# The gating projection with the inner dimension outermost: x loaded transposed, eight PSUM banks, small loads behind the large ones

## The chip, the cores and the metric

One Trainium2 chip, one of its cores. The metric is the device time of one execution in microseconds (us); shorter is better. Times inside the kernel are counted from the start of the span of a profiled execution.

## The reference, cut to what matters

One layer of a streaming encoder over 1024 frames of 1024 channels. The change touches the first projection alone, columns 0 to 511 of `w_in`, and how its operands reach the chip.

```
h    = rms_norm(x, norm_mix)                 # x: 1024 x 1024
proj = h @ w_in                              # 1024 x 2304
z_sgu, z_s5, z_qkv = split(proj, [512, 768])
o_a = sgu_mixer(gelu(z_sgu), ...)            # spatial gating: u * (W v + b), v = rms_norm(...)
o_b = s5_mixer(z_s5, lam, log_dt, b, c, ...) # diagonal state space, its powers made of lam and dt
o_c = band_attention(q, k, v, ...)
x   = x + rms_norm(concat[o_a, o_b, o_c]) @ w_out
x   = x + hier_moe(rms_norm(x))              # 16 experts
```

## The kernel before, in words

The program is one straight line. Python code emits instructions tile by tile; a scheduler then sets, when the program is built, the order in which each engine takes its instructions, by dependencies and program order. On the chip each engine takes its list in that order: an instruction that waits holds up those behind it on its engine. Up to the attention no order is written out by hand.

Matrix products in float32 are made of three passes (`mm3`, L129 to L132): an operand a is split into a high part (ScalarE copy to the short float, `split` L126) and a low residual (VectorE subtraction, L127), and high times high, high times low and low times high are summed in PSUM.

The first projection (`sgu_proj`, L190 to L223) goes over eight blocks `tb` of 128 frames, in pairs `pr`. For a pair, TensorE transposes 16 tiles of 128 x 128 of x against an identity matrix (L205, into `hTp`, PSUM tag `big`, three buffers of two banks). ScalarE turns `hTp` into the high part `hTh` with the gain (L209) and VectorE makes the residual `hTl` (L210). Then one block is one accumulation over all eight slices k of the inner dimension (24 matmuls of 512 columns) into one bank `pj` of the tag `acc` (two buffers of one bank), and ScalarE evicts it through GELU with the frame's scale `rs` into `gz` (L195). The scale comes from the squares of x (ScalarE, L218) and a short VectorE iteration (`rsqrt`).

Loads are issued from the SyncE queue: two blocks of x, the four pieces of the weight (`rw`, L173), six more blocks of x. Eight small loads go through ScalarE's queue. Each DMA uses one of eight completion counters in turn and waits for the one that used it before.

Behind the projection in program order stand:
- `r8` (L229 to L234): a one-column-block matmul `rsp` of `rs`, copied by VectorE. It orders the scales for the state space part.
- the preparation of the state space part (L308 to L434), some 60 VectorE instructions on `lam`, `dt`, `s5c`, `ak`, `scr`, `kap`, `bcm`, with two sines (L359) and two exponentials (L317, L376) on ScalarE, each of which has its own function table to load.
- the state space projection (four accumulations `pj` of 24 matmuls, evicted as `zT` by ScalarE, L446).
- the gating itself (`sgu`, L249 to L289), a generator whose pieces are emitted between those accumulations: VectorE sums (L259) and normalises `gz` into `vn` (L263), ScalarE and VectorE split it into `vh` and `vl`, TensorE multiplies with the mask weights `wsh` into `sgup` (12 matmuls, L270), VectorE forms `oa` (L275). It runs twice (`tq`).
- the k, q and v projections, between which the state space scan (`s5`) is emitted, attention, the output product, the experts.

Of the kernel before, what the change touches and what calls it, by code (L numbers as in the profile page):

```python
# [4 lines left out]
F32 = mybir.dt.float32  # L5
# [9 lines left out]
S = 1024  # L15
D = 1024
# [15 lines left out]
def trunk(tc, A, dbg=None, upto="all"):  # L32
# [35 lines left out]
    def slot(name, shape, dt=F32, far=None):  # L68
        far = name in FAR if far is None else far
        return slots.tile(shape, dt, name=name, tag="far" if far else "slot", bufs=FARS if far else SLOTS)  # L70
# [4 lines left out]
    def big(name, shape, dt=F32):  # L75
        return psum.tile(shape, dt, name=name, tag="big", bufs=3)

    def acc(name, shape, dt=F32):
        return psum.tile(shape, dt, name=name, tag="acc", bufs=2)
# [19 lines left out]
    def f32(ap):  # L99
        return ap.bitcast(F32)  # L100
# [37 lines left out]
    def load_x(tb):  # L138
        t = slot("xt", [128, D])
        sp.dma_start(t, x[tb * 128:(tb + 1) * 128, :])  # L140
        return t
# [6 lines left out]
    def junk():  # L148
        return work.tile([128, D], BF, name="junk", tag="w2")
# [17 lines left out]
    def load_w(c0, n, far=()):  # L167

        his, los = [], []
        per = 1024 // n  # L170
        for r in range(KD // per):
            rw = raw("rw", [128, per, n])
            sp.dma_start(rw, w_in[r * per * 128:(r + 1) * per * 128, c0:c0 + n]  # L173
                         .rearrange("(k p) c -> p k c", p=128))
            h = slot("wh", [128, per, n], F32R, far=r in far)
            l = slot("wl", [128, per, n], F32R, far=r in far)
            split(h, l, rw)
            his += [h[:, i] for i in range(per)]
            los += [l[:, i] for i in range(per)]
        return his, los  # L180

    def proj(out, sel, w, ks=range(KD)):
        his, los = w
        for k in ks:
            mm3(out, hT[k][:, sel], lT[k][:, sel], his[k], los[k], k == ks[0], k == ks[-1])

    gz = []
    rs = const("rs", [128, NT])

    def sgu_proj(tb):  # L190
        a = acc("pj", [128, 512])
        proj(a, slice(tb * 128, (tb + 1) * 128), W["sgu"])
        if tb % 2 == 0:
            gz.append(slot("gz", [128, 2, 512]))
        act.activation(gz[tb // 2][:, tb % 2], a, AF.Gelu_apprx_tanh, scale=rs[:, tb:tb + 1])  # L195

    W = {}
    xs = {0: load_x(0), 1: load_x(1)}
    for pr in range(4):
        for kq in range(2):  # L200
            p = big("hTp", [128, 4, 256])
            for q in range(2):
                for k in range(4):
                    kk = 4 * kq + k
                    pe.transpose(p[:, k, q * 128:(q + 1) * 128], xs[2 * pr + q][:, kk * 128:(kk + 1) * 128], ident)  # L205
            for k in range(4):
                kk = 4 * kq + k
                sl = slice(pr * 256, (pr + 1) * 256)
                act.activation(hT[kk][:, sl], p[:, k], AF.Copy, scale=gmix[:, kk:kk + 1])  # L209
                dve.scalar_tensor_tensor(lT[kk][:, sl], p[:, k], gmix[:, kk:kk + 1], f32(hT[kk][:, sl]),  # L210
                                         op0=OP.mult, op1=OP.subtract)
        if pr == 0:
            W["sgu"] = load_w(0, 512)
            for tb in range(2, NT):
                xs[tb] = load_x(tb)
        ss = small.tile([128, 2], F32, name="ssx")
        for q in range(2):
            act.activation(junk(), xs[2 * pr + q], AF.Square, accum_out=ss[:, q:q + 1])  # L218
        rsqrt(rs[:, 2 * pr:2 * pr + 2], ss, 2, 1.0 / D)
        if pr == 3:  # L220
            W["s5"] = load_w(512, 256)
        sgu_proj(2 * pr)
        sgu_proj(2 * pr + 1)  # L223
    W["k"] = load_w(1280, 512)

    div8, mod8 = const("div8", [128, 16]), const("mod8", [128, 8])
# [10 lines left out]
    row256 = const("row256", [128, 256])  # L237
    gsgu, glub = row256, row256
    wsr = slot("wsr", [128, 4, 128])
    act.dma_start(gsgu, bass.AP(tensor=A["sgu_norm"].tensor, offset=A["sgu_norm"].offset, ap=[[0, 128], [1, 256]]))  # L240
    sgb = const("sgb", [128, 4])
    act.dma_start(sgb, A["sgu_bT"])
    act.dma_start(wsr, A["sgu_wT"])
    pool.memset(wsr[64:128, :, 0:64], 0.0)
    wsh = slot("wsh", [128, 2, 4, 128], F32R)
    split(wsh[:, 0], wsh[:, 1], wsr)
# [58 lines left out]
            v = v.rearrange("p (a b c) -> p a b c", a=shape[1], b=shape[2])  # L305
        return v

    lam = const("lam", [128, 2, NG])  # L308
    act.dma_start(lam, A["lam2"])
    ldt = const("ldt", [128, NG])  # L310
    act.dma_start(ldt, bass.AP(tensor=A["log_dt"].tensor, offset=A["log_dt"].offset, ap=[[0, 128], [1, NG]]))
    bc_in = slot("bc_in", [128, 4, NG, 16])
    act.dma_start(bc_in, A["bc2"])
    d5 = const("d5", [16, NG])
    act.dma_start(d5, A["s5_dT"])
    dt = const("dt5", [128, NG])
    act.activation(dt, ldt, AF.Exp)  # L317
    th = const("th5", [128, NG])
# [310 lines left out]
    W["q"] = load_w(768, 512, (0, 1))  # L629
    qt_ = qk_proj("qt", W["q"])  # L630
    W["v"] = load_w(1792, 512, (3,))
    gqk = const("gqk", [128, 2])
    act.dma_start(gqk, A["qk2"])
    gq = const("gq", [128, 1])
    dve.scalar_tensor_tensor(gq, gqk[:, 0:1], 64 ** -0.5, gqk[:, 1:2], op0=OP.mult, op1=OP.mult)

# [969 lines left out]
def layout(inputs):  # L1606

    import numpy as np
    i = {k: np.asarray(v) for k, v in inputs.items()}
    f = np.ascontiguousarray  # L1610
    o = {"x": i["x"], "w_in": i["w_in"][0]}
    lr, li = i["s5_lambda_re"][0].T, i["s5_lambda_im"][0].T
    o["lam2"] = np.stack([np.concatenate([lr, lr]), np.concatenate([li, li])], 1)
    br, bi = (i[n][0].transpose(1, 0, 2) for n in ("s5_b_re", "s5_b_im"))
    cr, ci = (i[n][0].transpose(2, 0, 1) for n in ("s5_c_re", "s5_c_im"))
    o["bc2"] = np.stack([np.concatenate(p) for p in ((br, bi), (bi, br), (cr, ci), (ci, cr))], 1)
    o["log_dt"] = i["s5_log_dt"][0]
    o["s5_dT"] = i["s5_d"][0].reshape(16, 16).T
    o["glu_w"] = i["s5_glu_w"][0]
    o["glu_b"] = i["s5_glu_b"][0]  # L1620
    o["sgu_norm"] = i["sgu_norm"][0]
    o["sgu_bT"] = i["sgu_b"][0].T
    o["sgu_wT"] = i["sgu_w"][0].transpose(2, 0, 1)
    o["qk2"] = np.stack([np.concatenate([i[n][0]] * 2) for n in ("q_norm", "k_norm")], 1)
    o["norm_ffn"] = i["norm_ffn"][0]
    o["gT"] = np.stack([i[n][0].reshape(8, 128).T for n in ("norm_mix", "out_norm", "norm_ffn")], 1)
    o["w_out"] = i["w_out"][0]
    o["w_router"] = np.concatenate([i["router_group_w"][0], i["router_expert_w"][0].transpose(1, 0, 2).reshape(D, 16)], 1)
    o["b_router"] = np.concatenate([i["router_group_b"][0], i["router_expert_b"][0].reshape(16)])
    o["w_gu"] = np.concatenate([i["w_gate"][0], i["w_up"][0]], 2)  # L1630
    o["w_down"] = i["w_down"][0]
    rb = i["rel_bias"][0]
    rx = np.concatenate([np.repeat(rb[:, 512:], 639 - 255, axis=1), rb[:, 129:512][:, ::-1]], axis=1)

    o["relT"] = np.stack([rx[:, 127 - q:767 - q] for q in range(128)], 1)
    return {k: f(v) for k, v in o.items()}
# [17 lines left out]
```

## Time and profile before

| | |
|---|---|
| three runs | 831.81, 834.27, 837.59 us (median 834.27) |
| the profiled execution | 835.0 us, its span 833.1 us |
| TensorE busy | 755.7 us, 91% of the span |
| VectorE busy | 530.1 us, 64% |
| ScalarE busy | 400.9 us, 48% |
| GpSimd busy | 200.4 us, 24% |
| moved by DMA | 111.31 MB, 134 GB/s over the span |

A span runs from the first to the last instruction; the execution's own time is 1.9 us longer. In the rows further down, a timeline row gives start, duration, engine, line, operation, tiles and shape, and in brackets how long the engine had been idle and which instruction ended that. Matmuls are pipelined: the distance between two starts is what one costs, not its duration. PE is TensorE, DVE VectorE, ACT ScalarE, POOL GpSimd, SPq SyncE's queue.

### The profile page before, as it was taken

The numbers are of one execution on the slowest core, as the hardware profiler recorded it, in microseconds if no ns is written. First come the engines' busy times: TensorE is split into PE (matmuls) and PEld (weight loads), VectorE is DVE, ScalarE is ACT, GpSimd is POOL, SyncE is SP. The second block draws the span as 40 slices with busy tenths as digits, with TensorE's granted clock in tenths as the row PEclk, the third lists the DMA queues.
The fourth block names the chain that finished last, engine by engine and source line by source line (L and its number), as shares of the span: only waits on it lengthen the run. The fifth ranks groups of instructions, "written<-read, shape, count | busy, mean of one in ns | idle before, by whom it ended". The sixth has DMA issues, their size and how long they took to land. (4 is left out here: it accounts for less than half of the span.)

```text
span 833.1 us, 13661 instructions
## 1 busy us (share of the span) xinstructions
PE 755.7 (91%) x5024; PEld 640.0 (77%) x5025; DVE 530.1 (64%) x1266; ACT 400.9 (48%) x751; POOL 200.4 (24%) x235
## 2 busy tenths in 40 slices
PE   5999998989999887888888999968899999999995
PEld 4878777868888777888887888747678778888884
DVE  5866799873651467787877544677675774575541
ACT  6763432223343467777774323434454654464441
POOL 0000245411410332212101121112242433243221
PEclk9999999999999989999999999998999999999998
DMA  8423011330000400001045323286889999899663
GB/s 312 138 57 102 6 15 15 54 114 0 2 1 1 126 26 2 1 27 52 2 132 188 140 101 127 76 306 201 286 283 279 328 349 315 223 308 309 130 154 54
DMA packets 56516, 111.31 MB, mean 134 GB/s; under 512 B 24272, under 2 KB 28880, under 8 KB 56432
## 3 DMA queue, kind: packets, MB, share of 16 engines
q1 hardware_dynamic: 46880, 84.14, 30.0%
q0 software_dynamic: 6480, 23.60, 11.9%
q10 hardware_dynamic: 3072, 2.49, 1.0%
q8 instruction: 47, 0.77, 0.4%
q14 instruction: 37, 0.30, 0.1%
HBM read 90.05 MB, written 20.17 MB: 132 GB/s over the span
## 5 line engine op out<-in xcount | busy, mean ns | idle before, releaser
L130 PE MATMUL pj<-wh,hTh 128*128 128x512 f32 x256 | 104.2, 408 | 0.4 <-ACT hTh L209 0.3
L131 PE MATMUL pj<-wl,hTh 128*128 128x512 f32 x256 | 101.6, 397 | 0.0
L132 PE MATMUL pj<-wh,hTl 128*128 128x512 f32 x256 | 100.5, 398 | 0.1
L130 PE MATMUL gup<-gh,hgh 128*128 128x256 f32 x304 | 89.8, 295 | 1.7 <-ACT hgh L1278 0.2
L132 PE MATMUL gup<-gh,hgl 128*128 128x256 f32 x304 | 86.8, 286 | 3.1 <-DVE hgl L1282 3.1
L131 PE MATMUL gup<-gl,hgh 128*128 128x256 f32 x304 | 86.0, 283 | 0.0
L1325 PE MATMUL yp<-rwd,hh 128*128 128x256 f32 (+1 forms) x264 | 84.4, 457 | 0.0
L977 DVE TENSOR_TENSOR gl<-rwg,gh 128x1024 fp32r<-128x1024 f32 x64 | 78.0, 1241 | 7.3 <-ACT gh L972 6.5
L972 ACT ACTIVATE gh<-rwg 128x1024 fp32r<-128x1024 f32 x64 | 64.1, 1052 | 1.4 <-ACTq L1581 0.4
L1325 PEld LDWEIGHTS yp<-rwd,hh 128*128 128x128 f32 x264 | 45.8, 190 | 23.2 <-issue 17.4
L130 PEld LDWEIGHTS gup<-gh,hgh 128*128 128x128 f32 x304 | 57.9, 191 | 6.1 <-ACT y L1334 5.2
L132 PEld LDWEIGHTS gup<-gh,hgl 128*128 128x128 f32 x304 | 58.2, 191 | 4.5 <-DVE hgl L1282 3.6
L131 PEld LDWEIGHTS gup<-gl,hgh 128*128 128x128 f32 x304 | 58.2, 191 | 0.1
L132 PEld LDWEIGHTS pj<-wh,hTl 128*128 128x128 f32 x256 | 48.1, 188 | 12.7 <-DVE hTl L210 1.3
L130 PEld LDWEIGHTS pj<-wh,hTh 128*128 128x128 f32 x256 | 48.5, 190 | 12.0 <-ACT hTh L209 1.3
L1337 POOL DMA_INDIRECT out<-y,ix x22 | 38.2, 1735 | 78.9 <-ACT y L1334 45.9
L127 DVE TENSOR_TENSOR ptl<-ps,pth 128x640 fp32r<-128x640 f32 (+2 forms) x53 | 39.7, 749 | 26.5 <-ACT pth L126 26.1
L131 PEld LDWEIGHTS pj<-wl,hTh 128*128 128x128 f32 x256 | 48.4, 189 | 10.4
L130 PE MATMUL po<-pth,v_h 128*64 128x128 f32 x236 | 47.8, 232 | 2.9 <-DVE oc L765 2.0
L1334 ACT ACTIVATE y<-yp 128x512 f32<-128x512 f32 (+1 forms) x44 | 21.6, 491 | 59.6 <-PE yp L1325 59.6
L1262 POOL DMA_INDIRECT hg<-h2d,ix x22 | 23.8, 1080 | 105.2 <-PE yp L1325 69.5
L732 PE MATMUL ps<-ident,st 128*128 128x128 f32 x240 | 38.5, 290 | 9.8 <-ACT st L723 9.2
(390 smaller groups left out, 1974.9 us busy)
## 6 DMA issues: line engine op xcount, KB each, us to landing
rwg<-in_w_gu SPq DMA_DIRECT2D x62, 512.0 KB, 9.0
rwd<-in_w_down SPq DMA_DIRECT2D x32, 512.0 KB, 6.6
rw<-in_w_in SPq DMA_DIRECT2D x18, 512.0 KB, 5.1
xt<-in_x SPq DMA_DIRECT2D x8, 512.0 KB, 9.2
rwo<-in_w_out SPq DMA_DIRECT2D x8, 512.0 KB, 4.6
xr<-in_x SPq DMA_DIRECT2D x8, 512.0 KB, 4.3
out<-x SPq DMA_DIRECT2D x8, 512.0 KB, 2.6
h2d<-h SPq DMA_DIRECT2D x8, 512.0 KB, 2.9
```

The source lines that it names most:

```text
L127: (eng_lo or dve).tensor_tensor(lo, src, f32(hi), op=OP.subtract)
L130: pe.matmul(out, ah, bh, start=first, stop=False)
L131: pe.matmul(out, ah, bl, start=False, stop=False)
L132: pe.matmul(out, al, bh, start=False, stop=last)
L732: pe.transpose(pp[:, b], st[:, b * 128:(b + 1) * 128], ident)
L972: act.activation(pc[1], pc[0], AF.Copy)
L977: eng.tensor_tensor(t, pc[0], f32(pc[1]), op=OP.subtract)
L1262: pool.indirect_dma_start(out=self.hg, out_offset=None, in_=h2d[:, :], in_offset=bass.IndirectOffsetOnAxis(ap=self.ix, axis=0))
L1325: pe.matmul(self.py[nb][0], self.hh[r], self.ex.d[r][:, ns], start=(r == 0), stop=(r == 1))
L1334: act.activation(self.y[:, ns], p, AF.Copy)
L1337: pool.indirect_dma_start(out=out[:, :], out_offset=bass.IndirectOffsetOnAxis(ap=self.ix, axis=0), in_=self.y, in_offset=None, compute_op= ...
```

## The change

The host lays x out a second time, transposed (`xT`). The projection then needs no transposes: slices of `xT` come by DMA, and `hTh`, `hTl` are made from SBUF. The loop over the inner dimension becomes the outer one: for each slice k all eight blocks `tb` are advanced by three matmuls, so that eight accumulations are open at once, in all eight PSUM banks (three buffers of `big` with two banks each, two of `acc`). GELU evictions follow at the end. x itself is loaded after the transposed copy, for the squares alone. The small loads move from ScalarE's queue to SyncE's, behind the large ones.

```
-    gz = []
+    gz = [slot("gz", [128, 2, 512]) for _ in range(NT // 2)]
-    def sgu_proj(tb):
-        a = acc("pj", [128, 512])
-        proj(a, slice(tb * 128, (tb + 1) * 128), W["sgu"])
...
-        act.activation(gz[tb // 2][:, tb % 2], a, AF.Gelu_apprx_tanh, scale=rs[:, tb:tb + 1])
-    xs = {0: load_x(0), 1: load_x(1)}
-    for pr in range(4):
-        for kq in range(2):
-            p = big("hTp", [128, 4, 256])
...
-                    pe.transpose(p[:, k, q * 128:(q + 1) * 128], xs[2 * pr + q][:, kk * 128:(kk + 1) * 128], ident)
...
-        sgu_proj(2 * pr)
-        sgu_proj(2 * pr + 1)
+    pj = [big("pj", [128, 2, 512]) for _ in range(3)]
+    pj = [t[:, i] for t in pj for i in range(2)] + [acc("pj", [128, 512]) for _ in range(2)]
+    for r in range(4):
+        rw = raw("rw", [128, 2, 512])
+        sp.dma_start(rw, w_in[r * 256:(r + 1) * 256, 0:512].rearrange("(k p) c -> p k c", p=128))
+        xT = []
+        for k in (2 * r, 2 * r + 1):
+            xT.append(slot("xt", [128, S]))
+            sp.dma_start(xT[-1], A["xT"][k * 128:(k + 1) * 128, :])
+        wh, wl = slot("wh", [128, 2, 512], F32R), slot("wl", [128, 2, 512], F32R)
+        for i in range(2):
+            k = 2 * r + i
+            g = gmix[:, k:k + 1]
+            split(wh[:, i], wl[:, i], rw[:, i])
+            for sl in (slice(0, 512), slice(512, S)):
+                act.activation(hT[k][:, sl], xT[i][:, sl], AF.Copy, scale=g)
+                dve.scalar_tensor_tensor(lT[k][:, sl], xT[i][:, sl], g, f32(hT[k][:, sl]), op0=OP.mult, op1=OP.subtract)
+            for tb in range(NT):
+                sel = slice(tb * 128, (tb + 1) * 128)
+                mm3(pj[tb], hT[k][:, sel], lT[k][:, sel], wh[:, i], wl[:, i], k == 0, k == KD - 1)
+    lam = const("lam", [128, 2, NG])
+    sp.dma_start(lam, A["lam2"])
...
+    bc_in = slot("bc_in", [128, 4, NG, 16])
+    sp.dma_start(bc_in, A["bc2"])
...
+    for tb in range(NT):
+        act.activation(junk(), load_x(tb), AF.Square, accum_out=ss[:, tb:tb + 1])
+    rsqrt(rs, ss, NT, 1.0 / D)
+    W["s5"] = load_w(512, 256)
+    for tb in range(NT):
+        act.activation(gz[tb // 2][:, tb % 2], pj[tb], AF.Gelu_apprx_tanh, scale=rs[:, tb:tb + 1])
     W["k"] = load_w(1280, 512)
...
-    act.dma_start(wsr, A["sgu_wT"])
+    sp.dma_start(wsr, A["sgu_wT"])
...
-    gqk = const("gqk", [128, 2])
-    act.dma_start(gqk, A["qk2"])
+    gqk = small.tile([128, 2], F32, name="gqk", tag="s16")
+    sp.dma_start(gqk, A["qk2"])
...
-    o = {"x": i["x"], "w_in": i["w_in"][0]}
+    o = {"x": i["x"], "xT": i["x"][0].T, "w_in": i["w_in"][0]}
```

The scheduler sets new orders for the first part of the program; from the transposes `s5u` on, TensorE, ScalarE and GpSimd have the same list as before, and VectorE too but for one small multiplication (`gq`) that has moved between two weight splits of the v projection. Three places follow. The numbers behind the names are buffers; what stands in brackets is which engines or DMA counters an instruction waits for.

VectorE, before, around the copy of `r8` (the end of the first projection): `bcm`, the last of the state space preparation, and the residuals `hTl` stand ahead of it, the first sums of the gating (ISA on `gz`) right behind.

```order
L420 TENSOR_TENSOR bcm_704<-bcm_704,s5c_621 128x256 [waits DVE_49]
L127 TENSOR_TENSOR wl_521<-rw_518,wh_520 128x1024 [waits DMAHW5_49,Activation_49]
L210 SCALAR_TENSOR_TENSOR hTl0_92<-hTp_459,gains_82,hTh0_84 128x256 [waits Activation_49]
...
L127 TENSOR_TENSOR wl_592<-rw_589,wh_591 128x1024 [waits DMAHW3_49,PE_49,Activation_49]
L234 COPY r8_609<-rsp_607 128x8 [waits PE_49]
L127 TENSOR_TENSOR wl_598<-rw_595,wh_597 128x1024 [waits DMAHW4_49,Activation_49]
L259 ISA vn_755,sv_753<-gz_219 128x256
```

VectorE, now, around the same copy, and where the gating's first sum stands:

```order
L231 TENSOR_TENSOR rsx_485<-rs_104,div8_481 128x128 [waits DVE_49]
L127 TENSOR_TENSOR wl_446<-rw_443,wh_445 128x1024 [waits DMAHW2_49,Activation_49]
L235 COPY r8_489<-rsp_487 128x8 [waits PE_49]
L342 TENSOR_TENSOR s5c_501<-tH_517,kio_522 128x144 [waits Pool_49]
L127 TENSOR_TENSOR wl_460<-rw_457,wh_459 128x1024 [waits DMAHW3_49,Activation_49]
L127 TENSOR_TENSOR wsh_498<-wsr_492,wsh_498 128x512 [waits DMAHW1_49,Activation_49]
...
L343 TENSOR_SCALAR s5c_501<-s5c_501 128x144 [waits DVE_49]
...
L412 TENSOR_TENSOR s5c_501<-kap_557,bc_in_386 128x256 [waits DVE_49]
L260 ISA vn_627,sv_625<-gz_100 128x256
```

Three of the four weight splits of the k projection, the split of `wsh` and 48 instructions of the preparation (from L342 to L412) have moved from ahead of the copy of `r8` to between it and the gating, where the fourth weight split stood before, too.

ScalarE, before, from the end of the first projection's GELU evictions on (the sines and exponentials stood between earlier evictions):

```order
L126 ACTIVATE wh_591<-rw_589 128x1024 [waits DMAHW3_49,PE_49]
L195 ACTIVATE gz_549<-pj_551,rs_100 128x512 [waits PE_49]
L126 ACTIVATE wh_597<-rw_595 128x1024 [waits DMAHW4_49]
L446 ACTIVATE zT0_725<-pj_727 128x512 [waits PE_49]
L126 ACTIVATE vh_756<-vn_755 128x1024 [waits DVE_49]
```

and now:

```order
L224 ACTIVATE gz_103<-pj_109,rs_104 128x512 [waits PE_49]
L126 ACTIVATE wh_459<-rw_457 128x1024 [waits DMAHW3_49]
L126 ACTIVATE wsh_498<-wsr_492 128x512 [waits DMAHW1_49,Pool_49]
...
L352 ACT_TABLE_LOAD
L352 ACTIVATE ak_527<-ak_527 128x288 [waits DVE_49]
L352 ACTIVATE scr_539<-scr_539 128x768 [waits DVE_49]
L369 ACT_TABLE_LOAD
L369 ACTIVATE s5c_501<-s5c_501 128x144 [waits DVE_49]
L439 ACTIVATE zT0_597<-pj_599 128x512 [waits PE_49]
L439 ACTIVATE zT0_597<-pj_676 128x512 [waits PE_49]
L126 ACTIVATE vh_628<-vn_627 128x1024 [waits DVE_49]
```

The sines and the exponential of the preparation now stand behind all evictions and ahead of the first `zT`.

TensorE, before, at the first product of the gating (`sgup`), in the third accumulation of the state space projection:

```order
L130 MATMUL pj_879<-hTh0_84,wh_514 128x512 [waits Activation_49]
L131 MATMUL pj_879<-hTl0_92,wh_514 128x512
L132 MATMUL pj_879<-hTh0_84,wl_515 128x512
L130 MATMUL sgup_782<-vh_756,wsh_618 128x256 [waits PE_49,Activation_49]
L130 MATMUL pj_879<-hTh1_85,wh_514 128x512
```

and now, at the same place:

```order
L130 MATMUL pj_751<-hTh6_90,wh_445 128x512
L131 MATMUL pj_751<-hTl6_98,wh_445 128x512
L130 MATMUL sgup_654<-vh_628,wsh_498 128x256 [waits Activation_49]
L132 MATMUL pj_751<-hTh6_90,wl_446 128x512
L130 MATMUL pj_751<-hTh7_91,wh_445 128x512
L131 MATMUL pj_751<-hTl7_99,wh_445 128x512
L132 MATMUL pj_751<-hTh7_91,wl_446 128x512
L130 MATMUL pj_819<-hTh0_84,wh_439 128x512
L131 MATMUL sgup_654<-vl_629,wsh_498 128x256 [waits DVE_49]
```

The first `sgup` has moved from behind the 51st matmul of that projection to behind the 68th.

## Rows read from the trace of the kernel before

**Rows 1.** The page, busy us (share of the span) and instructions of TensorE.

```profile
PE 755.7 (91%) x5024; PEld 640.0 (77%) x5025; DVE 530.1 (64%) x1266; ACT 400.9 (48%) x751; POOL 200.4 (24%) x235
```

**Rows 2.** Timeline of TensorE, the first projection, and the state space projection's first matmul.

```profile
9.90 3.67 PE L205 MATMUL hTp<-ident,xt 128*128 128x128 f32 x16 [9.90 <-DVE ident L146]
...
25.80 2.79 PE L205 MATMUL hTp<-ident,xt 128*128 128x128 f32 x24
...
50.40 0.39 PE L132 MATMUL pj<-wh,hTl 128*128 128x512 f32 x1
50.63 0.39 PE L130 MATMUL pj<-wh,hTh 128*128 128x512 f32 x1
...
65.97 0.28 PE L232 MATMUL rsp<-mod,rsx 128*128 128x8 f32 x2
66.91 0.51 PE L130 MATMUL pj<-hTh,wh 128*128 128x512 f32 x1 [0.66 <-ACT gz L195]
```

**Rows 3.** DMA issues from 0 to 1 us and from 1 to 2 us: median us to landing.

```profile
xt<-in_x SPq DMA_DIRECT2D x1, 512.0 KB, 3.8
...
xt<-in_x SPq DMA_DIRECT2D x2, 512.0 KB, 4.4
```

**Rows 4.** Timeline of VectorE, preparation of the state space part, then the gating.

```profile
36.00 0.30 DVE L355 TENSOR_TENSOR ak<-s5c 128x144 f32<-128x144 f32 x1
...
37.21 0.56 DVE L349 TENSOR_TENSOR s5c<-tH,cio 128x384 f32<-128x384 f32 x1
...
42.35 0.31 DVE L375 TENSOR_TENSOR s5c<-lr,kio 128x144 f32<-128x144 f32 x1
...
45.88 0.17 DVE L377 COPY rad<-s5c 128x16 f32<-128x16 f32 x1 [1.15 <-ACT s5c L376]
...
52.64 0.41 DVE L420 TENSOR_TENSOR bcm<-bcm,s5c 128x256 f32<-128x256 f32 x1
...
63.88 3.50 DVE L127 TENSOR_TENSOR wl<-rw,wh 128x1024 fp32r<-128x1024 f32 x3 [4.89 <-ACT wh L126]
...
68.98 0.42 DVE L259 CUSTOM_DVE_ANT_0 vn<-gz 128x256 f32<-128x256 f32 x1
...
75.46 1.23 DVE L127 TENSOR_TENSOR vl<-vn,vh 128x1024 fp32r<-128x1024 f32 x1 [1.13 <-ACT vh L126]
81.52 2.16 DVE L275 SCALAR_TENSOR_TENSOR oa<-sgup,sgb,gz 128x128 f32<-128x128 f32 x8 [4.84 <-PE sgup L132]
```

**Rows 5.** Timeline of ScalarE, sine, table load, exponential, weight splits, last eviction, `vh`.

```profile
43.00 0.84 ACT L359 ACTIVATE scr<-scr 128x768 f32<-128x768 f32 x1
...
44.23 1.28 ACT L376 ACT_TABLE_LOAD   x1
45.52 0.33 ACT L376 ACTIVATE s5c<-s5c 128x144 f32<-128x144 f32 x1
...
62.80 2.94 ACT L126 ACTIVATE wh<-rw 128x1024 fp32r<-128x1024 f32 x3
66.17 0.69 ACT L195 ACTIVATE gz<-pj,rs 128x512 f32<-128x512 f32 x1 [0.43 <-PE pj L132]
...
74.37 1.06 ACT L126 ACTIVATE vh<-vn 128x1024 fp32r<-128x1024 f32 x1 [1.03 <-DVE vn L263]
```

**Rows 6.** Timeline of TensorE, first matmul of both gating products; the scan's longest wait.

```profile
78.72 0.28 PE L130 MATMUL sgup<-vh,wsh 128*128 128x256 f32 x1
...
92.54 0.39 PE L130 MATMUL sgup<-vh,wsh 128*128 128x256 f32 x1 [1.72 <-ACT vh L126]
...
141.37 0.49 PE L546 MATMUL s5y<-w,f 128*128 128x128 f32 x2 [3.71 <-DVE w L538]
```

**Rows 7.** Windows: busy PE, PEld, DVE, ACT, POOL; granted clock; DMA share; GB/s.

```profile
142.00:143.00 1.00, 1.00 (x7) 1.00 (x6) 1.00 (x2) 0.00 (x0) 0.00 (x0) 0.50 0.00 0
...
145.00:146.00 1.00, 1.00 (x10) 1.00 (x9) 0.90 (x3) 0.25 (x1) 0.69 (x3) 0.90 0.00 0
...
100.00:110.00 10.00, 10.00 (x61) 8.48 (x60) 8.78 (x17) 6.75 (x17) 4.39 (x5) 1.00 0.01 2
```

More of the change, by code (lines that the diff above doesn't have):

```diff
@@ L185, in proj @@
             mm3(out, hT[k][:, sel], lT[k][:, sel], his[k], los[k], k == ks[0], k == ks[-1])
-    gz = []
+    gz = [slot("gz", [128, 2, 512]) for _ in range(NT // 2)]
     rs = const("rs", [128, NT])
-    def sgu_proj(tb):
-        a = acc("pj", [128, 512])
-        proj(a, slice(tb * 128, (tb + 1) * 128), W["sgu"])
-        if tb % 2 == 0:
-            gz.append(slot("gz", [128, 2, 512]))
-        act.activation(gz[tb // 2][:, tb % 2], a, AF.Gelu_apprx_tanh, scale=rs[:, tb:tb + 1])
-    W = {}
@@ L198, in trunk @@
-    xs = {0: load_x(0), 1: load_x(1)}
-    for pr in range(4):
-        for kq in range(2):
-            p = big("hTp", [128, 4, 256])
-            for q in range(2):
-                for k in range(4):
-                    kk = 4 * kq + k
-                    pe.transpose(p[:, k, q * 128:(q + 1) * 128], xs[2 * pr + q][:, kk * 128:(kk + 1) * 128], ident)
[L206 to L221, printed above, removed]
-        sgu_proj(2 * pr)
-        sgu_proj(2 * pr + 1)
@@ new lines, in trunk @@
+    lam = const("lam", [128, 2, NG])
+    sp.dma_start(lam, A["lam2"])
+    ldt = const("ldt", [128, NG])
+    sp.dma_start(ldt, bass.AP(tensor=A["log_dt"].tensor, offset=A["log_dt"].offset, ap=[[0, 128], [1, NG]]))
+    bc_in = slot("bc_in", [128, 4, NG, 16])
+    sp.dma_start(bc_in, A["bc2"])
+    d5 = const("d5", [16, NG])
+    sp.dma_start(d5, A["s5_dT"])
+    ss = const("ssx", [128, NT])
+    for tb in range(NT):
+        act.activation(junk(), load_x(tb), AF.Square, accum_out=ss[:, tb:tb + 1])
@@ L239, in trunk @@
     wsr = slot("wsr", [128, 4, 128])
-    act.dma_start(gsgu, bass.AP(tensor=A["sgu_norm"].tensor, offset=A["sgu_norm"].offset, ap=[[0, 128], [1, 256]]))
+    sp.dma_start(gsgu, bass.AP(tensor=A["sgu_norm"].tensor, offset=A["sgu_norm"].offset, ap=[[0, 128], [1, 256]]))
     sgb = const("sgb", [128, 4])
-    act.dma_start(sgb, A["sgu_bT"])
-    act.dma_start(wsr, A["sgu_wT"])
+    sp.dma_start(sgb, A["sgu_bT"])
+    sp.dma_start(wsr, A["sgu_wT"])
     pool.memset(wsr[64:128, :, 0:64], 0.0)
@@ L306, in tmp @@
         return v
[L308 to L315, printed above, removed]
     dt = const("dt5", [128, NG])
```

## The prediction

> **What bounds the kernel now.** The page comes first: TensorE is busy for 91% of the span [rows 1], so what counts is when each stage of it can begin. Then its timeline at the start. It does nothing until 9.90 us, transposes, and ends the first projection at 65.97 [rows 2]. The 192 matmuls of that projection start 0.233 us apart (50.40 to 50.63) [rows 2], which makes 44.8 of the 56.1 us; the rest is transposes and a slow beginning. What the reader is to see next is that VectorE's timeline in the same stretch is not idle: the state space preparation (`s5c` to `bcm`, 36.00 to 52.64) runs there, under the projection's matmuls, and is over before the gating's first sum at 68.98 [rows 4]. So two chains end near 69 us: TensorE's, which the change shortens, and VectorE's, which it reorders. The question is which is late afterwards.
>
> **What the change removes on TensorE.** Of the 64 transposes the first 16 fill 9.90 to about 13.3 [rows 2], 0.21 us each; the other 48 cost 2.79/24 = 0.116 each [rows 2], 5.6 us. Now the first matmul needs one weight piece and one slice of `xT`. The first load of 512 KB took 3.8 us from its issue at 0.75, and the pair in flight had a median of 4.4, so the second took 5.0 from about 1.2 [rows 3]: they landed near 4.6 and 6.2. The new order is weight piece, slice, slice, with no small loads in between; I take 4.6 and 5.9. ScalarE's half slice (0.6 us, the size of an eviction [rows 5]) gives a first matmul at about 6.65, VectorE's residual a steady run from 7.35. TensorE begins at the lower of its two levels (1.2 GHz), as behind its wait at 141.37, where the granted clock was 0.50 at 142 and 0.90 on the mean of 145 to 146, so low for about 3.8 us [rows 6, 7]. By 10.4 some 8 matmuls are done, and 184 x 0.233 = 42.9 put the end, call it T, at **53.4**, 12.6 us before 65.97. Later slices come faster than they are used: a slice and its half of a weight piece are one and a half loads, 2.4 us by that spacing of 1.6, and feed 24 matmuls, 5.6 us. Range of T: 52 to 55.5 by the landing.
>
> **What it moves on VectorE and ScalarE.** VectorE's list has the copy of `r8` right behind `rsx`. That copy waits for the matmul `rsp`, which stands behind the whole projection on TensorE. Everything behind it on VectorE, the preparation included, therefore waits for T, although VectorE has nothing else to do for more than 10 us before. Before, the preparation stood ahead of that copy. From T on, step by step:
> The last eviction and `rsp` take 0.65 us, as 65.97 to the last GELU's start at 66.17 and its 0.69 suggest [rows 2, 5]: copy at 54.05.
> ScalarE then splits the k weights, 0.98 each, and `wsh` (half the size, about 0.6) [rows 5]; VectorE follows with four residuals at 1.17 (3.50 for three) and one half-size one [rows 4]: the first waits for ScalarE until 55.1, the last ends near 60.4.
> The first rotation on 128x144: four instructions took 1.21 (36.00 to 37.21) [rows 4], ten about 3.0: 63.4. The second on 128x384: 5.14 (37.21 to 42.35) [rows 4]: 68.5. ScalarE can only then do the sine (0.84), load the table (1.28), do the exponential (0.33) [rows 5]: 71.0.
> `rad` to the last `bcm` took 45.88 to 53.05 [rows 4], with one weight residual (1.15) and two `hTl` (an estimate of 0.4 each) between them: 5.2 left, 76.2.
> Gating: 68.98 to 74.37, when `vh` could start, is 5.4, and `vh` 1.06 [rows 4, 5]: **`vh` is ready at 82.7**, and `vl` 1.23 later [rows 4]. Before it was ready at 75.43, and the product began at 78.72 [rows 6], on TensorE's order, with 3.3 us to spare.
>
> **What TensorE does meanwhile.** The state space projection starts at about 54.3, 12.6 us early. Its third accumulation needs the bank of the first, whose eviction `zT` stands on ScalarE behind the exponential, at 71.0 + 0.6: after 48 matmuls (65.5) TensorE stands still for 6 us. It does 20 more, the first eight at half clock, to 78.1, and meets the first `sgup`, which waits for `vh`: 4.6 us more. The 12.6 us are gone, and the product is 4.0 us late on 78.72.
> Both waits are longer than the 3.71 us behind which the clock was halved [rows 6, 7], so I count about 3.75 us at half clock from 82.7 on. Five long matmuls and half of the eleven short ones double: the product ends near 87.4 instead of 85.5. `oa` began at 81.52 [rows 4]: 5.9 late. From there to the second product 11.0 us pass (81.52 to 92.54) [rows 4, 6] on VectorE's list, which is the same as before; TensorE has only 23 matmuls left for that stretch, idles some 5 us, and is at half clock again for the second product, another 1.1. Of the transposes `s5z` four more, and a matmul of the k projection, now stand behind it: 0.9. That makes, rounded, **8.0 us late** where the equal lists begin, and TensorE is busy for 10.00 of 10 us from 100 on [rows 7], with nothing to catch up in.
> Bounds of this term: without any half clock 3.9 + 0.9 = 4.8; with T at its late end 10.
>
> **A rule against the half-clock terms.** The rows put 0.50 behind a wait of 3.71 us [rows 6, 7]. The Trainium skill, page "TensorE: Matmul & The Clock Gate", Part 1, says that the ramp is under 1% of a typical span and that one should not fit a cold count. By that rule the sum would be 4.8 late, by the row 8.0; both are under 1% of this span, so the rule can't choose, and I go by the row.
>
> **A rule against eight open banks.** The last slice closes the eight accumulations 0.70 us apart (three matmuls), and an eviction takes 0.69, less pipelining [rows 2, 5], so evictions keep pace and only the last is exposed. The Trainium skill, page "Perfetto Trace Analysis", Optimizing Tensor Performance, says that independent groups should rotate through different banks so that one's eviction overlaps the next one's matmuls. By it nothing is left to rotate into: eight evictions of 0.6 in a row would put `rsp` and all behind it 4 us later. No row here shows such a pile-up; it is a rival below.
>
> **Edits at nothing.** Small loads behind large: `lam` and its kin now land at about 20 us instead of 6, and their first users wait for T anyway; the loads for the gating come some 10 us before T; if they didn't, each would cost its 4 to 5 us [rows 3]. Eight issues leave ScalarE's queue at the start, when it waits for data. `gqk` goes behind the last v weight on SyncE; VectorE waits for it between two v splits, but its place in the queue is passed while the k or q projection runs; uncovered it would be one landing, up to 5 us, and I take 0. x is loaded for the squares behind twelve loads and four small ones; at 1.6 us a load the twentieth has landed near 38 us and the scales are ready near 40, ahead of the first eviction at T - 4.9 = 48.5. Twice the reading of x costs only that. The other squares, weights and evictions are the same in number.
>
> **The sum.** The profiled execution took 835.0, of which the median of the runs, 834.27, is 0.7 less. 835.0 + 8.0 = 843.0, on the median's scale **842.3**: the projection ends 12.6 us earlier, and 20.6 are lost behind it.
>
> **Rivals.**
> The gain carries through: 835.0 - 12.6 - 0.7 = 821.7. For it speaks that TensorE is the busiest engine and the stage is 100% its own. It needs `vh` by about 70 us, when TensorE reaches it; VectorE would have to do 28 us of its list in 16, or its preparation ahead of the copy of `r8`, and the order says otherwise. Chance 0.07.
> The clock stays full at the two products: 839.1. Against it the row at 142. Chance 0.18.
> The first slices land late, which makes the kernel clearly slower: seven loads now go out at once, where before two did. If the DMA engines share themselves among all seven, the first pair lands with the seventh, six spacings of 1.6 later, TensorE starts near 15, T is about 62, and the end 850. It beats the forecast from one spacing on. Against it: of the pair at the start the first landed 1.6 before the second, so loads go one behind another [rows 3]. Chance 0.06. This is also the case in which the change doesn't do what it says.
> The eviction pile-up: 846.3. Chance 0.06.
> Forecast: 0.63, with 840 to 845 as its own range.
>
> **How the numbers follow.** A measurement of this kernel tells about 1% from no change: under 825.9 is faster, over 842.6 slower. The forecast's centre lies just at the upper line, so its 0.63 is split, 0.33 within and 0.30 over; the full-clock case is within. Faster 0.07, within 0.51, slower 0.42. The range, 836.5 to 847, reaches from the full-clock case with the earliest T to the pile-up, and leaves out the carried gain and the shared loads.
>
> **What would show it.** First matmul near 6.7; the last of the projection near 53.4, 0.233 apart throughout; VectorE idle from about 40 until `r8`; then `s5c` at 54, `rad` behind the exponential near 71, first gating sum near 76; TensorE idle near 65 to 71.6 for `zT` and near 78 to 82.7 for `vh`, with a granted clock of 0.50 behind. I am wrong if the preparation runs before the projection's end, if `vh` is there by 75, or if the lateness at `s5u` is made up by the end of the scan.

## The result, and the profile after

| | before | after |
|---|---|---|
| median of 4 runs each, us | 834.38 (831.81 to 837.59) | 844.50 (843.23 to 846.37) |
| profiled execution, its span, us | 835.0, 833.1 | 843.86, 842.1 |
| mean granted clock of TensorE | 0.974 | 0.962 |

The change makes the kernel slower: ratio 1.0115, 95% interval 1.0076 to 1.0153. The forecast was 842.3 in 836.5 to 847.0.

The page's row of busy engines, which answers to [rows 1]: TensorE has 4.4 us less work (755.7 to 751.3) in a span that is 9.0 us longer, so it stands idle for 13.4 us more than before.

```profile
PE 751.3 (89%) x4960; PEld 637.4 (76%) x4961; DVE 523.1 (62%) x1221; ACT 396.5 (47%) x737; POOL 196.5 (23%) x235
```

The DMA issues from 0 to 1 us and from 1 to 2 us, with their median us to landing, for [rows 3]: the first weight piece lands in 4.0 us and the two slices behind it in a median of 5.2 (4.8 and 5.6 one by one), one behind the other, not all together.

```profile
rw<-in_w_in SPq DMA_DIRECT2D x1, 512.0 KB, 4.0
...
xt<-in_xT SPq DMA_DIRECT2D x2, 512.0 KB, 5.2
```

TensorE's timeline at the places of [rows 2] and [rows 6]: start, duration, engine, line, operation, tiles, and in brackets the idle time before and what ended it.

```profile
6.93 0.79 PE L130 MATMUL pj<-wh,hTh 128*128 128x512 f32 x1 [6.93 <-ACT hTh L205]
7.52 0.63 PE L131 MATMUL pj<-wl,hTh 128*128 128x512 f32 x1
7.95 0.63 PE L132 MATMUL pj<-wh,hTl 128*128 128x512 f32 x1
...
52.53 0.40 PE L132 MATMUL pj<-wh,hTl 128*128 128x512 f32 x1
53.48 0.39 PE L233 MATMUL rsp<-mod,rsx 128*128 128x8 f32 x2 [0.56 <-ACT gz L224]
54.12 0.50 PE L130 MATMUL pj<-hTh,wh 128*128 128x512 f32 x1 [0.26 <-DVE r L235]
...
71.29 0.80 PE L130 MATMUL pj<-hTh,wh 128*128 128x512 f32 x1 [5.71 <-ACT zT L439]
...
82.43 0.58 PE L130 MATMUL sgup<-vh,wsh 128*128 128x256 f32 x1 [4.25 <-ACT vh L126]
...
97.88 0.58 PE L130 MATMUL sgup<-vh,wsh 128*128 128x256 f32 x1 [5.69 <-ACT vh L126]
...
109.09 1.03 PE L456 MATMUL s5u<-ident,z 128*128 128x128 f32 x8
```

The `s5u` of the trace of before:

```profile
101.50 1.04 PE L463 MATMUL s5u<-ident,z 128*128 128x128 f32 x8
```

The first projection begins at 6.93, and its last matmul starts at 52.53. At a distance of 0.23 it is over near 52.8; before the change `rsp` followed without idle time at 65.97: some 13.2 us are gained. `rsp` now waits 0.56 for an eviction and starts at 53.48, so 12.5 us are left there, and 12.8 at the first matmul of the state space projection (54.12 against 66.91). Then TensorE stands still three times for 4 to 6 us, for `zT` and twice for `vh`. The first `sgup` is 3.7 us later than at 78.72, the first `s5u`, from which the lists are equal, 7.6 us later than before (109.09 against 101.50).

VectorE's timeline, for [rows 4]:

```profile
36.65 0.29 DVE L231 TENSOR_TENSOR rsx<-rs,div 128x128 f32<-128x128 f32 x1
36.86 1.22 DVE L127 TENSOR_TENSOR wl<-rw,wh 128x1024 fp32r<-128x1024 f32 x1
53.91 0.17 DVE L235 COPY r<-rsp 128x8 f32<-128x8 f32 x1 [15.83 <-PE rsp L233]
53.99 0.30 DVE L342 TENSOR_TENSOR s5c<-tH,kio 128x144 f32<-128x144 f32 x1
...
70.79 0.17 DVE L370 COPY rad<-s5c 128x16 f32<-128x16 f32 x1 [1.53 <-ACT s5c L369]
75.62 0.41 DVE L260 CUSTOM_DVE_ANT_0 vn<-gz 128x256 f32<-128x256 f32 x1
...
86.86 2.16 DVE L276 SCALAR_TENSOR_TENSOR oa<-sgup,sgb,gz 128x128 f32<-128x128 f32 x8 [3.23 <-PE sgup L132]
```

The same step of the first rotation in the trace of before, whose later steps [rows 4] shows:

```profile
32.14 0.30 DVE L349 TENSOR_TENSOR s5c<-tH,kio 128x144 f32<-128x144 f32 x1
```

VectorE idles 15.8 us ahead of the copy of `r8`, with the preparation (`s5c` to `bcm`) behind it in its list. Its first rotation began at 32.1 before; now it begins at 54.0, and the gating's first sum moves from 68.98 to 75.62. ScalarE, for [rows 5]:

```profile
48.84 5.17 ACT L224 ACTIVATE gz<-pj,rs 128x512 f32<-128x512 f32 x8 [10.86 <-PE pj L132]
...
68.28 0.84 ACT L352 ACTIVATE scr<-scr 128x768 f32<-128x768 f32 x1 [4.69 <-DVE scr L351]
69.14 1.28 ACT L369 ACT_TABLE_LOAD   x1
70.43 0.32 ACT L369 ACTIVATE s5c<-s5c 128x144 f32<-128x144 f32 x1
70.66 1.07 ACT L439 ACTIVATE zT<-pj 128x512 f32<-128x512 f32 x2
81.32 1.06 ACT L126 ACTIVATE vh<-vn 128x1024 fp32r<-128x1024 f32 x1 [9.59 <-DVE vn L264]
```

The first `zT` stands behind sine, table and exponential, as the list said, and frees TensorE's bank only at 71. Windows of [rows 7]'s form (busy time of PE, PEld, DVE, ACT, POOL, granted clock, DMA share, GB/s) give the clock behind these waits:

```profile
72.00:73.00 1.00, 1.00 (x4) 0.81 (x3) 1.00 (x7) 0.00 (x0) 0.00 (x0) 0.50 0.00 0
...
83.00:84.00 1.00, 1.00 (x4) 0.81 (x3) 0.63 (x1) 0.00 (x0) 0.00 (x0) 0.50 0.00 0
...
99.00:100.00 1.00, 1.00 (x6) 0.86 (x5) 0.08 (x1) 0.00 (x0) 0.00 (x0) 0.50 0.09 30
```

It is at the lower level (1.2 GHz) each time. From the first `sgup` to `oa` 4.43 us pass (82.43 to 86.86), before 2.80 (78.72 to 81.52): 1.6 us lost. From the first `sgup` of the second product to the first `s5u`, TensorE has the same 52 matmuls in both kernels; they take 11.21 us (97.88 to 109.09), before 8.96 (92.54 to 101.50): 2.25 us more.

### The profile page after: what moved, and what is told of

Its sections match the earlier page's. It is cut to its first block, busy times and chain, and to the rows that moved or that the text cites. A ratio compares the mean times of both kernels' runs of the same rounds, so it can differ in the third digit from the quotient of the medians.

```text
span 842.1 us, 13491 instructions
## 1 busy us (share of the span) xinstructions
PE 751.3 (89%) x4960; PEld 637.4 (76%) x4961; DVE 523.1 (62%) x1221; ACT 396.5 (47%) x737; POOL 196.5 (23%) x235
## 5 line engine op out<-in xcount | busy, mean ns | idle before, releaser
L1318 PE MATMUL yp<-rwd,hh 128*128 128x256 f32 (+1 forms) x264 | 86.1, 464 | 0.0
L1318 PEld LDWEIGHTS yp<-rwd,hh 128*128 128x128 f32 x264 | 46.6, 193 | 23.8 <-issue 17.8
L131 PE MATMUL po<-ptl,v_h 128*64 128x128 f32 x236 | 46.1, 227 | 0.6 <-DVE ptl L127 0.6
```

Source lines behind the costliest of these rows:

```text
L131: pe.matmul(out, ah, bl, start=False, stop=False)
L1318: pe.matmul(self.py[nb][0], self.hh[r], self.ex.d[r][:, ns], start=(r == 0), stop=(r == 1))
```

## The experiments

Two theories stood against each other. A, the prediction's: the preparation stands behind the end of the first projection in VectorE's list, and so `vh` and all behind it are late. B: the loss comes from the work that the change adds (eight open banks, x read twice, contention). Each ratio is against runs of the kernel before on the same chip; their medians were 834.50 (e1 to e4), 834.24 (e5 to e8) and 836.89 us (e9), and 834.38 beside the change. What is said against the change itself compares medians of separate sets of runs.

### e1: the preparation ahead, all else kept

The block of the gating's small loads is written behind the preparation. The loads stay on SyncE's queue; the list alone was to change.

```
-    gsgu, glub = row256, row256
-    wsr = slot("wsr", [128, 4, 128])
...
-    split(wsh[:, 0], wsh[:, 1], wsr)
...
     dve.tensor_tensor(dg, bc(d5[:, :, None], [16, NG, 16]), ...)
+    gsgu, glub = row256, row256
+    wsr = slot("wsr", [128, 4, 128])
...
+    split(wsh[:, 0], wsh[:, 1], wsr)
     side.append(sgu())
```

> Everything of the change is kept, all small loads too; only the block of the gating's small loads with the split of wsh is written behind the state space preparation, so that VectorE's list now has the whole preparation ahead of the copy of r8, and ScalarE's sines and exponential stand ahead of the GELU evictions. Theory A (the preparation behind the end of the first projection is what is late): the projection still ends near 53.4, rad is done before 50, the first gating sum runs near 60, vh is ready near 66.5 and the first sgup starts near 67.5 instead of 82.4, with a wait under 1 us on vh; no wait of several us for zT; 821 to 827 us, 823 likeliest. Rival B (the loss comes from elsewhere: eight open banks, twice the reading of x, contention): 840 us or more, whatever the list says.

Measured: 825.98 us (823.89 to 829.93) beside 834.50, ratio 0.9905 (0.987 to 0.994); 18.5 us faster than the change. VectorE's timeline of this kernel, then TensorE's:

```profile
42.27 0.18 DVE L361 COPY rad<-s5c 128x16 f32<-128x16 f32 x1 [1.11 <-ACT s5c L360]
...
54.51 0.17 DVE L235 COPY r<-rsp 128x8 f32<-128x8 f32 x1 [6.88 <-PE rsp L233]
...
60.74 0.42 DVE L251 CUSTOM_DVE_ANT_0 vn<-gz 128x256 f32<-128x256 f32 x1
```

```profile
54.08 0.39 PE L233 MATMUL rsp<-mod,rsx 128*128 128x8 f32 x2 [0.56 <-ACT gz L224]
...
67.90 0.32 PE L130 MATMUL sgup<-vh,wsh 128*128 128x256 f32 x1
...
81.70 0.39 PE L130 MATMUL sgup<-vh,wsh 128*128 128x256 f32 x1 [2.83 <-ACT vh L126]
```

`rad` is done at 42.27 instead of 70.79, the first sum stands at 60.74 instead of 75.62, and the first `sgup` has no idle time before it. The wait for `zT` is gone. B falls: banks, double reading and loads are all there, and the kernel is faster than before the change.

### e2: the gating's three loads back on ScalarE's queue

```
-    sp.dma_start(gsgu, ...)
+    act.dma_start(gsgu, ...)
-    sp.dma_start(sgb, A["sgu_bT"])
-    sp.dma_start(wsr, A["sgu_wT"])
+    act.dma_start(sgb, A["sgu_bT"])
+    act.dma_start(wsr, A["sgu_wT"])
```

> The change with three of the eight small loads, those of the gating (sgu_norm, sgu_bT, wsr), back on ScalarE's queue; nothing else is undone. In VectorE's list two thirds of the preparation, up to the second rotation, now stand ahead of the copy of r8, the rest and the four k-weight residuals behind it; the exponential stands behind the evictions. Theory A: the first rotation runs from about 24 us, rad near 57, the first gating sum near 64.5, vh near 71, first sgup near 71 (before 78.72, after 82.43), so 7 to 8 us earlier than before: 825 to 831 us, 828 likeliest, between the two kernels' lists as its preparation is. Rival B: 840 us or more.

Measured: 832.62 us (829.71 to 833.50), ratio 0.9966 (0.9939 to 0.9994). About half of the preparation comes ahead and the time falls to 11.9 us below the change, but the size was missed: the first `sgup` came at 74.73, not 71. VectorE waited 10.2 us for `wsh` with the first rotation behind it, since `wsr` is issued between the squares on ScalarE, and the projection ended 2.8 us later than in the change: 1.2 by the first matmul, 8.13 instead of 6.93 behind two small loads, the rest about half in a longer slow start (to 13.8 instead of 10.9) and half in a distance of 0.233 between matmuls instead of 0.229.

```profile
36.08 0.69 DVE L127 TENSOR_TENSOR wsh<-wsr,wsh 128x512 fp32r<-128x512 f32 x1 [10.22 <-ACT wsh L126]
...
59.38 0.17 DVE L370 COPY rad<-s5c 128x16 f32<-128x16 f32 x1 [0.41 <-ACT s5c L369]
```

### e3: the copy of r8 on ScalarE

```
-    dve.tensor_copy(r8, r8p)
+    act.activation(r8, r8p, AF.Copy)
```

> The change with the copy of r8 made by ScalarE, behind the eviction it waits for anyway; VectorE's list is otherwise the same, with the preparation in the same place. Theory A as the prediction put it (VectorE waits at the copy) taken alone: VectorE is free from 36.7 us on, the preparation runs under the projection, about 823 us. Theory A2 (the place in the list counts, and the copy is only the first of several that wait for the projection's end: the third k-weight residual, behind a split that ScalarE does after the last eviction, is the next): VectorE waits 15 us or more all the same, now at that residual, vh is ready near 82.5, 843 to 846 us.

Measured: 844.16 us (843.26 to 845.94), ratio 1.0114 (1.0062 to 1.0166): no change, as A2 said. VectorE's timeline shows who stops it now:

```profile
39.29 0.30 DVE L342 TENSOR_TENSOR s5c<-tH,kio 128x144 f32<-128x144 f32 x1
54.90 1.23 DVE L127 TENSOR_TENSOR wl<-rw,wh 128x1024 fp32r<-128x1024 f32 x1 [15.31 <-ACT wh L126]
```

The preparation's first instruction runs at 39.29, the second stands behind weight residuals whose splits ScalarE makes after the last eviction. The copy named by the trace was the first of several waits for the same end.

### e4: the kernel before, with the preparation put behind

```
     dt = const("dt5", [128, NG])
     act.activation(dt, ldt, AF.Exp)
+    dt_, dt = dt, const("dt6", [128, NG])
+    dve.scalar_tensor_tensor(dt, bc(r8[:, 0:1], [128, NG]), 0.0, dt_, op0=OP.mult, op1=OP.add)
```

> The kernel before, with none of the change, but with one small multiplication of 128x16 added that makes the step size dt depend on the copy of r8 (it adds zero times r8); so the whole preparation stands behind the end of the first projection here too. Theory A: the projection ends at 66 as before, the copy at 66.6, two residuals, 1 us of small steps, the two rotations 8.2, sine, table and exponential 2.5, 5.2 to the last bcm, 5.4 and 1.06 to vh: vh near 92.5 instead of 75.4; the first sgup, which the list sets behind 68 matmuls as in the changed kernel, is 14 us late, the equal lists 15 to 17: 848 to 853 us. Rival B (the preparation's place costs little, the other parts of the change do): under 840 us.

Measured: 850.91 us (849.82 to 852.45), ratio 1.0196 (1.0144 to 1.0248): 16.4 us slower by the list alone, in the old loop. TensorE's timeline has the change's three waits:

```profile
80.71 0.50 PE L130 MATMUL pj<-hTh,wh 128*128 128x512 f32 x1 [2.68 <-ACT zT L448]
...
91.85 0.39 PE L130 MATMUL sgup<-vh,wsh 128*128 128x256 f32 x1 [4.68 <-ACT vh L126]
...
107.30 0.58 PE L130 MATMUL sgup<-vh,wsh 128*128 128x256 f32 x1 [5.78 <-ACT vh L126]
```

### e5: all small loads first, on ScalarE's queue

```
+    lam = const("lam", [128, 2, NG])
+    act.dma_start(lam, A["lam2"])
...
+    act.dma_start(d5, A["s5_dT"])
     hT = [local(f"hTh{k}", [128, S], F32R) for k in range(KD)]
...
-    sp.dma_start(lam, A["lam2"])
...
-    sp.dma_start(wsr, A["sgu_wT"])
+    act.dma_start(wsr, A["sgu_wT"])
```

> The change without its third part: xT from the host and eight banks stay, the seven small loads of the start go back to ScalarE's queue, where they are issued first (the one of the q and k norms stays where the change put it). VectorE's list has the whole preparation ahead of the copy of r8, the four k-weight residuals right behind it, and TensorE's list has the first sgup behind 51 matmuls of the state space projection, as before the change. Theory A: the first matmul comes 1.5 to 2.5 us later than 6.93, since the small loads (one of 512 KB) take the DMA engines first; the projection ends at 55 to 57; vh near 68, first sgup near 68.5, 10 us earlier than before the change: 823 to 829 us. So of the change only the place of the small loads in program order costs, by the list it leads to. Rival B: still 838 us or more, because the eight evictions or the double reading of x cost.

Measured: 825.34 us (824.53 to 826.62), ratio 0.9894 (0.9823 to 0.9966). With the third part taken back, but for the load of `gqk`, the other two are worth 8.9 us; so in the change it is the place of the small loads that costs. The first matmul was delayed by 0.4 us only, not by 1.5 to 2.5:

```profile
7.29 0.80 PE L130 MATMUL pj<-wh,hTh 128*128 128x512 f32 x1 [7.29 <-ACT hTh L214]
...
69.02 0.28 PE L130 MATMUL sgup<-vh,wsh 128*128 128x256 f32 x1
```

### e6: small loads behind large, alone

In the kernel before, eight times `act.dma_start` becomes `sp.dma_start`.

> The third part of the change alone: the kernel before, with its eight small loads on SyncE's queue, behind the large ones. VectorE's list still has the preparation ahead of the copy of r8, but for its last step, and mixed with the residuals of x. Theory A (late small loads are no cost in themselves as long as the list keeps the preparation under the projection): first sgup within 3 us of 78.72, 832 to 842 us. Rival C (the late landing itself costs, in any loop): 845 us or more.

Measured: 833.83 us (830.23 to 836.01), ratio 0.9989 (0.9959 to 1.0019): no change. C falls, late small loads cost nothing where the list keeps the preparation under the projection. The first `sgup` even came 3.2 us earlier, at 75.49, 2.1 of it because the transposes began at 7.81 instead of 9.90; at the end of the kernel 0.7 us of it are left.

### e7: the host's transposition with the old loop

```
-                    pe.transpose(p[:, k, ...], xs[2 * pr + q][...], ident)
+    def load_xT(pr):
+        for kq in range(2):
+            xTs[pr, kq] = slot("xt", [128, 4, 256])
+            sp.dma_start(xTs[pr, kq], xTv[:, 4 * kq:4 * kq + 4, pr * 256:pr * 256 + 256])
...
+            p = xTs[pr, kq]
```

> The first part of the change alone, and the good list: xT from the host, but the loop of the kernel before (blocks outermost, two accumulators in two banks in turn, x read for the squares between), small loads on ScalarE's queue, the gating's block behind the preparation as in the first experiment. It can't finish a block before all weights have landed, near 12 us; from there 0.233 us a matmul: the projection ends at 54 to 56.5, the first sgup near 70: 825 to 831 us, 828 likeliest, within 3 us of the first experiment's 826. Then the eight open banks are worth at most some 2 us of the 12. Rival D (the inner dimension outermost is what brings the early end): the projection ends at 60 or later, 833 us or more.

Measured: 835.43 us (832.15 to 840.42), ratio 1.0013 (0.9973 to 1.0052): A's number was missed, D's is right.

```profile
12.31 1.22 PE L130 MATMUL pj<-wh,hTh 128*128 128x512 f32 x2 [12.31 <-ACT wh L126]
...
60.20 0.28 PE L239 MATMUL rsp<-mod,rsx 128*128 128x8 f32 x2
```

The matmuls are 0.233 us apart here too; the projection ends 6.1 us later than in e1 because it starts 5.3 us later, at 12.31: its first weight piece stands behind two loads of `xT` and the small loads, and ScalarE can split it only at 11.20. So about half of the 12 us comes from the earlier start. Whether that needs the new order of the loops, or only the weight ahead of `xT` among the loads of the old loop, no run shows. The first `sgup` was at 75.22, 3.5 us earlier than before. Of that lead 1.7 us were left at the first `s5u` and about 2 at 600 us. Then, in the experts, TensorE waited 3.50 us for gathered rows (`hg`, at 609.34; before 1.41) and had a granted clock of 0.50 behind it (before 1.00); at 615 us it was 1.5 us late.

### e8: e1 with the first loads in halves

```
+        if r == 0:
+            sp.dma_start(rw[:, 0], w_in[0:128, 0:512])
+            sp.dma_start(xT[0][:, 0:512], A["xT"][0:128, 0:512])
+            sp.dma_start(xT[0][:, 512:S], A["xT"][0:128, 512:S])
+            sp.dma_start(rw[:, 1], w_in[128:256, 0:512])
```

> The first experiment's kernel (preparation ahead, 826), with the first weight piece and the first slice of xT loaded in halves of 256 KB, the halves that the first matmuls need in front. Expected: first matmul near 5 instead of 6.97, all matmuls behind it 0.233 apart as the slices come faster than they are used, the projection's end near 52 instead of 54.1, first sgup near 66: 822 to 826 us, 824 likeliest. Rival: two more DMAs in front delay the later slices, or vh is now what is late (it was just in time before): no change, 826.

Measured: 822.23 us (820.60 to 825.01), ratio 0.9861 (0.9786 to 0.9935). This version beats both kernels. The first matmul starts at 5.12 and `rsp` at 52.55, 1.5 us earlier than in e1. Against the expectation the matmuls behind it are not 0.23 apart throughout: the slow start lasts until 10.8.

```profile
5.12 0.79 PE L130 MATMUL pj<-wh,hTh 128*128 128x512 f32 x1 [5.12 <-ACT hTh L210]
...
66.37 0.32 PE L130 MATMUL sgup<-vh,wsh 128*128 128x256 f32 x1
```

### e9: work for TensorE during the waits

```
-            a = acc("pj", [128, 512])
+            a = big("pj", [128, 2, 512])[:, 0] if i == 1 else acc("pj", [128, 512])
```

> The change, with two of the four accumulations of the state space projection in banks of the tag big instead of acc, so that TensorE need not wait for the first zT. Its list then puts most of one k-projection accumulation (20 matmuls) ahead of the first sgup; VectorE's list still has the preparation behind the copy of r8, and vh is still ready near 82.4. Theory A (what is lost is TensorE's idle time at zT and vh, since it has nothing to catch up in later): some 20 to 25 matmuls, 5 us, are done in the waits and saved later: 837 to 841 us. Rival E (what counts is when the scan can start, which hangs on vh, oa and zT in VectorE's and ScalarE's lists; work done ahead on TensorE only moves the idle time): 842 to 846 us.

Measured: 837.91 us (833.34 to 840.04), ratio 1.0011 (0.9988 to 1.0034), 6.6 us better than the change by the medians and 4.9 by the profiled executions (838.94 against 843.86), in A's range, but not where it was expected:

```profile
72.37 0.80 PE L130 MATMUL pj<-wh,hTh 128*128 128x512 f32 x1 [5.71 <-ACT zT L439]
83.51 0.58 PE L130 MATMUL sgup<-vh,wsh 128*128 128x256 f32 x1 [4.46 <-ACT vh L126]
...
99.70 0.36 PE L130 MATMUL sgup<-vh,wsh 128*128 128x256 f32 x1
```

The waits for `zT` and the first `vh` stayed; the one ahead of the second product (5.69) is gone, filled with matmuls of the k projection. The first `s5u` comes at 110.18, 1.1 us later than in the change, but by then 59 matmuls of the k projection are done instead of 24 (35 at 0.233 us are 8.2 us). So rival E, by which only the start of the scan counts, falls: the idle time of TensorE is lost, and work drawn into it is won.

## Why the prediction was right

By its steps, forecast and then the traces:

| step | forecast | measured |
|---|---|---|
| first matmul | 6.65 | 6.93 |
| end of the first projection, T | 53.4 | 52.8 (`rsp` waits until 53.48) |
| scales ready | 40 | 36.6 |
| copy of `r8` | 54.05 | 53.91 |
| `rad` | 71.0 | 70.79 |
| first gating sum | 76.2 | 75.62 |
| `vh` ready | 82.7 | 82.4 |
| first `sgup` late by | 4.0 | 3.7 |
| `oa` late by | 5.9 | 5.3 |
| equal lists late by | 8.0 | 7.6 |
| execution late by | 8.0 | 8.9 |

The mechanism is shown, not only argued: taking the preparation's place away wins 18.5 us (e1), putting it into the kernel before costs 16.4 (e4), where the prediction's arithmetic, applied to that place in the expectation, gave 15 to 17.

One hit is partly luck. T came 0.6 us earlier than forecast, with matmuls 0.229 apart instead of 0.233, and from T to the copy of `r8` 1.1 us passed instead of 0.65, since `rsp` waited for an eviction; the two nearly cancel at the copy (54.05 and 53.91).

What was off:
- **The range's centre** was 2.2 us low on the median (842.3 against 844.5). About 1 us is in the executions themselves (8.9 instead of 8.0): 0.4 us less than forecast were lost up to `s5u`, 1.3 more behind it, in a lateness that moves between 4.3 and 9.9 us through attention and experts. It rises most in the experts, from 5.6 to 8.3 us, around a wait for gathered rows (`hg`): TensorE waits longer for them and then runs at the half clock, as the rows below show, first before the change and then after it. Why the rows came later is not shown. The other 1.3 is where the profiled executions lie among their runs: of before 0.7 above the median used, of after 0.6 below its own. The median lies above 842.6, the prediction's own line for slower, to which it gave 0.42, less than the 0.51 for within.

```profile
610.30 1.12 PE L1273 MATMUL hgp<-ident,hg 128*128 128x128 f32 x8 [1.41 <-DMA hg<-h2d,ix]
612.00:613.00 1.00, 1.00 (x6) 0.66 (x5) 1.00 (x2) 0.10 (x1) 0.00 (x0) 1.00 0.42 86
...
616.88 1.13 PE L1266 MATMUL hgp<-ident,hg 128*128 128x128 f32 x8 [2.45 <-DMA hg<-h2d,ix]
620.00:621.00 1.00, 1.00 (x4) 0.82 (x3) 0.90 (x4) 0.00 (x0) 0.00 (x0) 0.50 0.06 25
```

- **Small loads behind large, among the edits at nothing.** This step failed in its reason. By landing times it holds: `lam` landed at 19.2 and `ldt` at 20.4, and e6 shows no cost. The step says that their first users wait for T; they didn't: ScalarE made `dt` at 20.44, and VectorE's small steps up to `tL` ran from 22.5 to 23.8. Only the rotations stood behind T. But the three loads of the gating, by their place and queue, are what sets the preparation behind the projection in the list: with their block later (e1) or on ScalarE's queue (e2, e5) the list changes, and the time by 12 to 19 us. Why the scheduler lays the list out so is not shown. The prediction took the list as given and so priced the total rightly; it laid the loss to the end of the projection and did not see which edit moved it.
- **Everything behind the copy of `r8` waits for T.** True of the list, but the copy alone is not the cause: e3 takes it away and the next wait for the same end takes its place, 15.3 us instead of 15.8.
- **"Nothing to catch up in"** was too strong. TensorE has the k projection to draw forward (e9, 6.6 us by the medians); the list as it stood didn't.
- **The half clock.** The rows bear out the terms: 1.6 us at the first product, where 1.9 were forecast, and 2.25 from the second to the first `s5u`, where 1.1 and 0.9 were. The rival at full clock (839.1) falls. It was also priced 0.8 us too high: the 0.9 for the transposes and the matmul that moved behind the second product is no loss at full clock, as the 52 matmuls of that stretch are the same in both kernels. The Trainium skill ("TensorE: Matmul & The Clock Gate", Part 1) puts the ramp under 1% of a typical span: these 3.9 us are 0.5% of this one, which agrees, and yet over two fifths of what the change did.
- **The pile-up** didn't come: eight evictions took 5.17 us, from 48.84 to 54.01, and so ran under the last slice's matmuls; the last of them ended some 1.2 us behind the projection, and `rsp` waited 0.56. The Trainium skill ("Perfetto Trace Analysis", Optimizing Tensor Performance) has independent groups rotate through different banks so that one's eviction overlaps the next one's matmuls; the trace agrees, for eight groups in eight banks that close three matmuls apart. What the prediction drew from it, that no bank is left to rotate into, cost those 0.56 us and not 4.

## What to carry to other kernels

An earlier end on the busiest engine is worth only what the engine that feeds its next stage can follow; look in the list of that engine at what stands behind the end that moves, and ask what it could have done while it waits. When the trace names one instruction as what holds an engine up, look at the ones behind it before you move it: they may wait for the same event. Small loads were cheap here where they landed late and dear where their place or queue changed the order in which the scheduler laid out the work; compare the lists after such an edit, and move the block in program order if they changed.

## What was not expected of the hardware

At the start of the kernel the matmuls are 0.43 us apart (7.52 to 7.95 in the rows above), up to 10.5 us, and 0.23 later, though the granted clock of that stretch reads 1.00:

```profile
8.00:10.00 2.00, 2.00 (x6) 1.59 (x6) 2.00 (x5) 2.00 (x5) 0.00 (x0) 1.00 1.04 416
```

Behind the later waits the same distance comes with a granted clock of 0.50. The trace's list of clock changes has its first entry, full speed, only at 10.76 us in the change and at 12.02 in e1, each time where the distance falls; ahead of it nothing is recorded, and the view prints 1.00. At the start, then, the distance between starts tells the level and the clock's row doesn't. This slow stretch was of different length in kernels that differ little: in the change the starts are 0.23 apart from 10.86 on, in e1, whose first matmul came at the same time (6.97), only from 12.15 on, and that is the 0.6 us by which e1's projection ended later.

Nor does the length of a wait alone tell the clock behind it. Behind 2.83 us ahead of e1's second product it read 1.00 (82 to 83 us); behind 1.62 us ahead of `rsp` in e5 it read 0.50, with matmuls 0.43 apart:

```profile
56.00:57.00 1.00, 1.00 (x4) 0.81 (x3) 0.78 (x1) 1.00 (x3) 0.00 (x0) 0.50 0.00 0
```
